# A decoder step in split float32: other gaps between the weight buffers and the operand tiles in SBUF

## The chip, the cores and the metric

The kernel runs on one core of a Trainium2 chip. The metric is the device time of one execution in microseconds; lower is better. Beside the times there is a profile of one execution, taken by the hardware profiler.

## What is computed

One inference step through two layers of a decoder, for a prompt of 256 positions and 8 samples of one position each, 264 columns in all, that share every weight. In short:

```python
def moba_gmlp_mixer(x, ...):          # layer 0
    z = rmsnorm(x, norm_g) @ w_in     # 1024 -> 2560: q, k, v, bu, bv
    a = moba_attention(q, k_all, v_all, pos)
    b_out = spatial_gating(gelu(bu), layer_norm(gelu(bv), sgu_gain), sgu_w, sgu_b)
    return x + concatenate([a, b_out]) @ w_out

def sb_pool_mixer(x, ...):            # layer 1
    z = rmsnorm(x, norm_g) @ w_in     # 1024 -> 2048: q, k, v, u
    c_out = stick_breaking_attention(q, k_all, v_all, pos)
    d_out = pool_mixer(pool_prev, u, pos, pool_w, pool_scale)
    return x + concatenate([c_out, d_out]) @ w_out

def conv_ffn(x, ...):                 # behind each mixer
    h = rmsnorm(x, norm_g)
    g = h @ w_gate                    # 1024 -> 2816
    a = gelu(causal_conv3(g)) * (h @ w_up)
    return x + a @ w_down             # 2816 -> 1024
```

A last rmsnorm follows. Everything is float32, and the caches and states of the samples are read and written besides.

## The kernel before

**Products.** Each large weight matrix is cut into blocks of 128 x 128, 1472 in all, and the activations lie transposed, 128 features by 264 columns. To keep float32 precision with TensorE's faster float32 form (F32R), each operand is split into a high part (h) and the rest (l), and each block takes three products that add up in one PSUM bank: l with xh, then h with xl, then h with xh (`run`, in the list `three`; in the first 30 blocks of layer 0 another order). A product is one load of 128 x 128 weights and one matmul of 264 columns; the profile shows both under L219, the line of the wrapper `TensorE.matmul`, as PEld and PE. The 1472 x 3 products follow one another without a loop in the program; ScalarE and VectorE split the weights of coming blocks meanwhile (L315, L320) and work on finished banks.

**The order of blocks** is fixed by `_phases`: projection in, out, gate and up (ff), and down (dn) of layer 0, then of layer 1, with 160, 64, 352, 176, 128, 64, 352 and 176 blocks. Within one, `m` is the output tile and `k` the input tile. In most of them k runs 0, 1, 2, ... for one m. Exceptions that the prediction uses: in dn the odd m take k from 2 to 21 and then 0 and 1; in the output projections the first 24 blocks take one k for four m in turn, k = 4, 5, 6, 7, 0, 1, and the next 8 take k = 2, 3 for each of these four m. There `catB` holds k = 4 to 7 and `catA` k = 0 to 3.

**Where operands lie.** SBUF is handed out pool by pool, in the order of the lines that open the pools: `con`, `rawp` (weights as loaded), `wsh` (four buffers of high parts), `gap1`, `wsl` (four buffers of low parts), `gap2`, `up` (24 buffers for most else: operand tiles, early weights, cache pages), then `pp` and `sm`. The pools gap1 and gap2 each hold one tile that nothing uses. A weight tile holds 8 blocks, each 128 columns wide and padded to WP = 144; block i of the program is block c = i mod 8 of its tile. An operand tile holds four rows (k mod 4), each 264 columns padded to TP = 272, and starts X0 = 7 columns in:

```python
WP = 144
X0 = 7
    def mv(name):
        return [f4(f"{name}_{x}", (P, 4, TP), F32R)[:, :, X0:X0 + T] for x in "hl"]
    def hl(tiles, k):
        return tiles[k // 4][0][:, k % 4, :], tiles[k // 4][1][:, k % 4, :]
```

The operand tiles are called xg (normalised input), catA and catB (mixer outputs) and a (gated activations), with _h and _l for the parts; wh and wl are the split weights.

Of the kernel before, what the change touches and what calls it, by code (L numbers as in the profile page):

```python
# [9 lines left out]
F32 = mybir.dt.float32  # L10
# [8 lines left out]
P = 128  # L19
# [187 lines left out]
def tile_decoder_step(ctx: ExitStack, tc: tile.TileContext, a):  # L207
# [21 lines left out]
    gap1 = ctx.enter_context(tc.tile_pool(name="gap1", bufs=1))  # L229
    wsl = ctx.enter_context(tc.tile_pool(name="wsl", bufs=4))  # L230
    gap2 = ctx.enter_context(tc.tile_pool(name="gap2", bufs=1))
# [48 lines left out]
    def late(dst, src):  # L280
        tc.keep_in_program_order(nc.sync.dma_start(dst, src))

    gap1.tile([P, 56], F32, name="gap1")
    gap2.tile([P, 32], F32, name="gap2")

    def wtiles(tt):
        return [p.tile([P, 8, WP], F32R, tag=f"w{x}", name=f"w{x}{tt}")[:, :, :P] for p, x in ((wsh, "h"), (wsl, "l"))]
# [1052 lines left out]
```

## Time and profile before

| | before |
|---|---|
| median of three runs | 590.23 us (589.93 to 590.53) |
| the profiled execution | 590.45 us, of it the span 588.7 us |
| granted TensorE clock, mean | 0.999 |
| HBM read and written | 117.65 MB and 3.96 MB |

The span runs from the first instruction to the last. A busy share is the part of the span in which an engine had an instruction under way. Matmuls are pipelined: one starts while the one before still drains, so the durations of single matmuls overlap and their sum exceeds the span. What one costs is the time from its start to the next one's start. In the chain of work that ended last, each step is followed back to what released it; a piece such as "115.50 190.29 PE mm L219 x1578" tells its start, its length, and how many instructions were merged into it. Rows of groups show "busy us, mean ns of one".

### The profile page before, as it was taken

The page shows a single profiled execution, that of the slowest core. Times are in us where ns is not written, and L with a number is a line of the kernel's source. Part 1 is how long each engine was busy: PE and PEld are TensorE (multiplying, and loading weights), DVE is VectorE, ACT ScalarE, POOL GpSimd, SP SyncE. Part 2 cuts the span into 40 slices and gives each one's busy share as a digit, 9 for nine tenths or more (in the row PEclk, how much of TensorE's full clock was granted, in tenths as well). Part 3 has the DMA queues.
Part 4 walks back from the last instruction along what each step waited for, and adds up shares of the span by engine and source line. Part 5 has one row for each costly group of instructions (what it writes and reads, how often), then busy time and mean ns, then how long its engine had stood idle before and what let it go on. Part 6 is the DMA issues. An engine that isn't in the chain of part 4 may idle for free.

```text
span 588.7 us, 12306 instructions
## 1 busy us (share of the span) xinstructions
PE 583.5 (99%) x4909; PEld 568.8 (97%) x4909; DVE 419.7 (71%) x740; ACT 344.5 (59%) x615; POOL 113.2 (19%) x108
## 2 busy tenths in 40 slices
PE   9999999999999999999999999999999999999997
PEld 8998979999999999999999897999999999999996
DVE  6999766878777777665659585588777777764442
ACT  7848955775555555644453476667656565665442
POOL 1410021222222222210120000132232323221010
PEclk9999999999999999999999999999999999999999
DMA  8997973554454545795567865254545454546501
GB/s 318 370 368 284 380 265 102 186 172 187 168 191 161 197 169 190 270 398 199 178 230 258 279 227 187 81 209 151 209 148 211 148 211 146 207 161 219 208 2 73
DMA packets 27707, 122.40 MB, mean 208 GB/s; under 512 B 3330, under 2 KB 4226, under 8 KB 16258
## 3 DMA queue, kind: packets, MB, share of 16 engines
q1 hardware_dynamic: 27648, 121.62, 57.3%
q8 instruction: 38, 0.62, 0.4%
q14 instruction: 19, 0.16, 0.1%
q10 hardware_dynamic: 2, 0.00, 0.0%
HBM read 117.65 MB, written 3.96 MB: 207 GB/s over the span
## 4 chain that ended last, share of the span: by engine, by line
PE 96%; ACT 1%; DMA 1%; DVE 0%; SPq 0%; issue 0%; DVEq 0%
PE mm L219 89%; PE sc L219 1%; PE pv_l L219 1%; PE pav L219 1%; DMA xw<-in_xw 1%; PE pt L222 1%; PE S L219 1%; PE Z L219 1%; ACT xg_h L421 0%; ACT wh L750 0%; DVE wl L751 0%; PE pf L219 0%; PE pm L219 0%; PE vtp_v L222 0%; SPq L386 0%; ACT wh L738 0%
## 5 line engine op out<-in xcount | busy, mean ns | idle before, releaser
L320 DVE TENSOR_TENSOR wl<-raw,wh 128x1024 fp32r<-128x1024 f32 x179 | 219.3, 1227 | 69.5 <-ACT wh L315 69.1
L315 ACT ACTIVATE wh<-raw 128x1024 fp32r<-128x1024 f32 x179 | 187.6, 1051 | 84.0 <-PE mm L219 75.7
L219 PE MATMUL mm<-xg_f_l,wh 128*128 128x264 f32 x704 | 198.5, 282 | 0.0
L219 PE MATMUL mm<-xg_f_h,wh 128*128 128x264 f32 x704 | 198.2, 282 | 0.0
L219 PE MATMUL mm<-xg_f_h,wl 128*128 128x264 f32 x704 | 198.0, 281 | 0.0
L219 PEld LDWEIGHTS mm<-xg_f_h,wl 128*128 128x128 f32 x704 | 132.7, 188 | 0.0
L219 PEld LDWEIGHTS mm<-xg_f_l,wh 128*128 128x128 f32 x704 | 131.7, 187 | 0.0
L219 PEld LDWEIGHTS mm<-xg_f_h,wh 128*128 128x128 f32 x704 | 131.6, 187 | 0.0
L613 POOL TENSOR_TENSOR wk<-wk 128x264 f32<-128x264 f32 x44 | 66.3, 1507 | 194.6 <-DVE wk L612 148.0
L219 PE MATMUL mm<-a_l,wh 128*128 128x264 f32 x352 | 99.3, 282 | 0.0
L219 PE MATMUL mm<-a_h,wh 128*128 128x264 f32 x352 | 99.1, 282 | 0.0
L219 PE MATMUL mm<-a_h,wl 128*128 128x264 f32 x352 | 99.1, 281 | 0.0
L219 PEld LDWEIGHTS mm<-a_h,wl 128*128 128x128 f32 x352 | 66.4, 189 | 0.0
L219 PEld LDWEIGHTS mm<-a_h,wh 128*128 128x128 f32 x352 | 65.9, 187 | 0.0
L219 PEld LDWEIGHTS mm<-a_l,wh 128*128 128x128 f32 x352 | 65.9, 187 | 0.0
L470 ACT ACTIVATE a_h<-wk 128x264 fp32r<-128x264 f32 x44 | 18.6, 424 | 73.8 <-POOL wk L613 73.8
L471 DVE TENSOR_TENSOR a_l<-wk,a_h 128x264 fp32r<-128x264 f32 x44 | 19.2, 437 | 42.0 <-ACT a_h L470 42.0
L219 PE MATMUL mm<-xg_h,wl 128*128 128x264 f32 x160 | 43.2, 292 | 0.2 <-DVE wl L751 0.2
L219 PE MATMUL mm<-xg_h,wh 128*128 128x264 f32 x160 | 42.6, 288 | 0.1
L219 PE MATMUL mm<-xg_l,wh 128*128 128x264 f32 x160 | 41.9, 283 | 0.0
L219 PE MATMUL mm<-xg_n_h,wl 128*128 128x264 f32 x128 | 37.8, 295 | 0.0
L219 PE MATMUL mm<-xg_n_h,wh 128*128 128x264 f32 x128 | 36.1, 282 | 0.0
(265 smaller groups left out, 900.0 us busy)
## 6 DMA issues: line engine op xcount, KB each, us to landing
raw<-in_w SPq DMA_DIRECT2D x89, 1024.0 KB, 4.9
K<-in_kt SPq DMA_DIRECT2D x32, 256.0 KB, 6.5
V<-in_vp SPq DMA_DIRECT2D x32, 256.0 KB, 6.4
raw<-in_w SPq DMA_DIRECT2D x3, 512.0 KB, 6.5
xw<-in_xw SPq DMA_DIRECT2D x3, 388.0 KB, 6.0
X<-in_x SPq DMA_DIRECT2D x4, 264.0 KB, 6.6
out_y<-y SPq DMA_DIRECT2D x3, 256.0 KB, 2.2
out_k<-k SPq DMA_DIRECT2D x1, 528.0 KB, 7.3
```

What stands on the lines that cost most here:

```text
L219: return self.keep(nc.tensor.matmul(*x, **k))
L222: return self.keep(nc.tensor.transpose(*x, **k))
L315: i = s.activation(h, src, AF.Copy)
L320: i = v.tensor_tensor(l, src, h.bitcast(F32), ALU.subtract)
L470: s.activation(h, src, AF.Copy)
L471: v.tensor_tensor(l, src, h.bitcast(F32), ALU.subtract)
L613: g.tensor_tensor(A, A, C, ALU.mult)
```

## The change

Two numbers change, the sizes of the two unused tiles, in float32 elements:

```diff
-    gap1.tile([P, 56], F32, name="gap1")
-    gap2.tile([P, 32], F32, name="gap2")
+    gap1.tile([P, 48], F32, name="gap1")
+    gap2.tile([P, 8], F32, name="gap2")
```

So in each partition the low weight parts move down by 32 bytes against the high ones, and `up`, `pp` and `sm` by 128 bytes. With the sizes above, x then lies 252 bytes, modulo 256, ahead of the weights that are loaded for the next product, for all three products of a block in which c and k agree modulo 4; before, these distances are 124, 124 and 92. No instruction is added, removed or moved on any engine, and no tile gets another size or another number of buffers.

## The prediction

> **What bounds the kernel now.** I read the page's busy shares first, then what TensorE waits for, then the chain that ended last.
>
> ```profile
> span 588.7 us, 12306 instructions
> PE 583.5 (99%) x4909; PEld 568.8 (97%) x4909; DVE 419.7 (71%) x740; ACT 344.5 (59%) x615; POOL 113.2 (19%) x108
> PEclk9999999999999999999999999999999999999999
> PE 96%; ACT 1%; DMA 1%; DVE 0%; SPq 0%; issue 0%; DVEq 0%
> PE mm L219 89%; PE sc L219 1%; PE pv_l L219 1%; PE pav L219 1%; DMA xw<-in_xw 1%; PE pt L222 1%; PE S L219 1%; PE Z L219 1%; ACT xg_h L421 0%; ACT wh L750 0%; DVE wl L751 0%; PE pf L219 0%; PE pm L219 0%; PE vtp_v L222 0%; SPq L386 0%; ACT wh L738 0%
> PE warm L219 <- PEq L1306: 0.8, 1, 0.8
> PE mm L219 <- DVE wl L751: 0.2, 1, 0.2
> ```
>
> TensorE is busy throughout at the full granted clock, it holds 96% of the chain, and its two rows of waits come to 1.0 us. No other engine needs watching. 89% of the span is one kind of work: the split products of L219, of which there are 1472 blocks x 3 = 4416. So the kernel's time is the number of products times the time from the start of one to the start of the next. Two long pieces of the chain give that step:
>
> ```profile
> 115.50 190.29 PE mm L219 x1578
> 396.19 185.22 PE mm L219 x1536
> ```
>
> 190.29 / 1578 and 185.22 / 1536 are both 120.6 ns. The change can matter only through these 120.6 ns, or through the short stretches that are not products.
>
> **What the change moves.** Every engine issues the same instructions in the same order before and after; only addresses differ, so no count and no queue enters the sum. All distances below are remainders by 256 bytes. A weight tile is 8 x 144 x 4 = 4608 bytes and a tile of `up` 4352 bytes, both whole multiples of 256, so every buffer of a pool has its pool's remainder. Call that of `wsh` 0. Then `wsl` goes from 224 to 192, and `up` from 224 + 128 = 96 (less 256) to 192 + 32 = 224. Block c of a weight tile lies 64 c further (144 x 4 = 576), row k of an operand tile 28 + 64 k further. Where c and k agree by remainder 4, as in about 1370 of the 1472 blocks, the three products of a block have x ahead of the weights that are loaded for the next product by:
>
> - first (weights l, operand xh; next h): 28 + 96 = 124 before, 252 after
> - second (h, xl; next h again): 124 before, 252 after
> - third (h, xh; next is l of block c + 1): 28 + 96 - 224 - 64 = 92 before, 252 after
>
> Does the trace say that this distance matters? It holds other distances already, in the blocks where c and k disagree. In the down projections the odd output tiles end with k = 0 and 1. The first projection of that kind starts with block 576; its second output tile has those two at blocks 618 and 619, where c is 2 and 3: two ahead, so the distances are 252, 252 and 220. Block 618 is 126 products after the first, at 236.87 + 126 x 0.1206 = 252.06 us:
>
> ```profile
> 236.87 0.28 PE L219 MATMUL mm<-a_h,wl 128*128 128x264 f32 x1
> ...
> 252.06 0.28 PE L219 MATMUL mm<-a_h,wl 128*128 128x264 f32 x1
> ```
>
> The view that groups lines gives the mean duration in the window 252.22 to 252.78 us, which holds just these six products, and in 253.68 to 254.23 us, which holds six with the usual distances:
>
> ```profile
> L219 PE MATMUL mm<-a_h,wh 128*128 128x264 f32 x2 | 0.6, 285 | 0.0
> L219 PE MATMUL mm<-a_l,wh 128*128 128x264 f32 x2 | 0.6, 284 | 0.0
> L219 PE MATMUL mm<-a_h,wl 128*128 128x264 f32 x2 | 0.6, 281 | 0.0
> ```
>
> ```profile
> L219 PE MATMUL mm<-a_l,wh 128*128 128x264 f32 x2 | 0.6, 282 | 0.0
> L219 PE MATMUL mm<-a_h,wl 128*128 128x264 f32 x2 | 0.6, 282 | 0.0
> L219 PE MATMUL mm<-a_h,wh 128*128 128x264 f32 x2 | 0.6, 282 | 0.0
> ```
>
> The loads that run beside them show it as well. Here are the rows of weight loads of those two windows, the unusual distances first:
>
> ```profile
> L219 PEld LDWEIGHTS mm<-a_h,wl 128*128 128x128 f32 x2 | 0.4, 190 | 0.0
> ...
> L219 PEld LDWEIGHTS mm<-a_h,wl 128*128 128x128 f32 x2 | 0.4, 188 | 0.0
> ```
>
> So a product and the load of the next weights do hinder each other, by a few nanoseconds, and the distance changes by how much. A duration is some 161 ns longer than the step (about 282 against 120.6), since it goes on while the next product streams; a nanosecond more of one I count as a nanosecond more of the other.
>
> The Trainium skill (TensorE: Matmul & The Clock Gate, "Step-by-step: what each phase is for") says that TensorE has two independent read ports into SBUF, so that loading the next weights takes no read bandwidth from the running product. The rows above (281 to 285 against 282, loads of 190 against 188) speak against it at this fine grain; by that rule alone the change would do nothing.
>
> **The sum.** By these rows, against the usual block:
>
> - First product at 252: 281 against 282, so -1 ns.
> - Second at 252: 284 against 282, so +2 ns.
> - Third at 252: the trace has no row of it. Below, it could be like the first at 252, -1 ns. Above, it could be like the third at 220, the nearest distance that there is, 285 against 282, so +3 ns. I take the middle, +1 ns, since one row has the right distance and the other the right product; both ends stay for the range.
>
> That is +2 ns a block, between 0 and +4, and x 1370 blocks: **+2.7 us, between 0 and +5.5**. The hundred blocks with other distances keep their mix, moved by 128 or so, and are put at nothing (the two in each odd tile of the down projections get 124, 124 and 124; 16 blocks x 5 ns are under 0.1 us).
>
> The other term is the data that moves along. Everything in `up` and behind it moves by 128 bytes, among it the tiles that the first loads fill, and the chain has one of these loads:
>
> ```profile
> 2.60 5.48 DMA xw<-in_xw
> raw<-in_w SPq DMA_DIRECT2D x89, 1024.0 KB, 4.9
> raw<-in_w SPq DMA_DIRECT2D x3, 512.0 KB, 6.5
> ```
>
> By the addresses that the program is built with, the 89 loads go to tiles that start 160 bytes behind a multiple of 256, the 3 to tiles in `up` that start on one, and 128 behind it after the change; the former are no slower for their size, so I put this at nothing. A twentieth of the 5.48 us in either direction would be 0.3 us. VectorE, ScalarE and GpSimd read the same tiles at moved addresses; TensorE hides them, having waited for one of them for 0.2 us in all.
>
> The profiled execution took 590.45 us: 588.7 of span and 1.75 around it, 0.2 above the median of 590.23. From the median, 590.23 + 2.7 = **593.0 us**.
>
> **The rivals.**
>
> *No change.* If what a load takes from a product is the same at every distance, only at another moment, the sum of a block stays. For it: the first two products at 252 come to 565 ns together against 564, so all of the forecast beyond 1 ns hangs on the third. Then 590.2, within 1.2 us.
>
> *Faster.* One distance for all three may settle into one rhythm, in which every product starts as the good ones do. For it: the first product at 252 is below its usual duration in the rows above, and single products come down to 279 (window 253.92 to 253.99 us):
>
> ```profile
> L219 PE MATMUL mm<-a_h,wh 128*128 128x264 f32 x1 | 0.3, 279 | 0.0
> ```
>
> Against it: the first product at 252 was followed by a slow one at the same distance. If all three were like the first, -3 ns x 1370 = -4.1 us: 586.1. If all were at 279, -3 x 3 x 1370 ns = -12 us: 578, the end of what this trace has. It decides at the point where the third product at 252 is more than 1 ns below its usual 282.
>
> The Trainium skill (the same page, "Back-to-back issue gap") gives N / 2.4 + 2.5 ns for products one behind the other, 112.5 ns for 264 columns, against the 120.6 ns measured. If the 8 ns between were all hindrance and 252 removed it, an estimate from that page would be 33 us less; no row here comes near it, since the shortest product is 3 ns below the usual one.
>
> *Clearly slower.* Slow products at 252 may feed each other when no good distance comes in between. The trace has a stretch of it. In the first output projection, the first product on catA is block 176, where c = 0; blocks 183, 184 and 185 are then three in a row at 252, 252, 220. They start seven blocks later and end where block 186 starts:
>
> ```profile
> 91.94 0.28 PE L219 MATMUL mm<-catA_h,wl 128*128 128x264 f32 x1
> ...
> 94.46 0.28 PE L219 MATMUL mm<-catA_h,wl 128*128 128x264 f32 x1
> ...
> 95.56 0.28 PE L219 MATMUL mm<-catA_h,wl 128*128 128x264 f32 x1
> ```
>
> 1.10 us / 9 is 122.2 ns a product, 1.6 more than 120.6 (within 1 ns for the rounding). 1.6 x 3 x 1370 is +6.6 us: 596.8. The worst single products, the second and third of block 618 (window 252.35 to 252.42 us), would, if all were so, give +4.5 x 4110 ns = +18 us: 609.
>
> ```profile
> L219 PE MATMUL mm<-a_l,wh 128*128 128x264 f32 x1 | 0.3, 287 | 0.0
> L219 PE MATMUL mm<-a_h,wh 128*128 128x264 f32 x1 | 0.3, 286 | 0.0
> ```
>
> **How the numbers follow.** The forecast, 0 to +4 ns a block with most of it above +1, gets 0.42 and the stretch at 252 with +6.6 us or more 0.14; no change 0.20; faster 0.24. A measurement of this kernel can tell some 0.2% from no change, 1.2 us. The forecast's lowest part falls within that and counts to "same" in exchange for what "no change" spreads upward, so faster 0.25, same 0.20, slower 0.55. The range has to reach the faster case at 586 and the slower one just past 597; all products at 279, and all at 286, are left out: 586 to 598.
>
> **What would show it.** The steps of the two long pieces of the chain in the changed profile: 121.3 ns for the forecast, 120.6 for no change, under 120.2 for faster, 122 for clearly slower. The mean durations by group: the wl group (first product) near 281, the second, on the l operand, near 284, the third near 283. The rest of the span should not move: the pieces sc, pv, pav and the start up to the first product within 0.3 us. I am wrong if the third product goes the other way than its neighbour at 220, or if the three settle into a rhythm that short stretches between other distances cannot show.

## The result, and the profile after

The changed kernel takes 587.02 us (586.67 to 587.46), the kernel before 590.23 us: a ratio of 0.9947, 95% interval 0.9933 to 0.9962. It is 0.5% faster, where 0.5% slower was forecast. The time is inside the range, near the rival "faster" (586.1).

The first page of the changed kernel, beside the lines shown of before:

```profile
span 585.6 us, 12306 instructions
PE 579.7 (99%) x4909; PEld 563.7 (96%) x4909; DVE 420.1 (72%) x740; ACT 344.3 (59%) x615; POOL 114.1 (19%) x108
PE 73%; DVE 13%; ACT 7%; POOL 4%; issue 2%; DMA 1%; SPq 0%; DVEq 0%; POOLq 0%; ACTq 0%
```

TensorE is as busy as before, but its share of the chain fell from 96% to 73%: somewhere the chain now leaves it. The span is 3.1 us shorter. The pieces of the chain say how fast the products follow one another, in their order of time:

```profile
115.21 86.01 PE mm L219 x720
243.47 60.73 PE mm L219 x506
394.16 86.01 PE mm L219 x720
522.42 55.71 PE mm L219 x464
```

86.01 / 720 is **119.5 ns** a product, against 120.6 before. All three products of a block got quicker: by the starts in the trace, in blocks in which c and k agree, the step behind the first fell from 120.4 to 119.6 ns, behind the second from 120.5 to 119.2, behind the third from 120.8 to 119.6. The mean durations in the groups of the page show less of it (last number; before they were 281 for the first, wl, and 282 for the other two):

```profile
L219 PE MATMUL mm<-xg_f_h,wh 128*128 128x264 f32 x704 | 197.8, 281 | 0.0
L219 PE MATMUL mm<-xg_f_h,wl 128*128 128x264 f32 x704 | 197.8, 281 | 0.0
L219 PE MATMUL mm<-xg_f_l,wh 128*128 128x264 f32 x704 | 197.5, 280 | 0.0
```

1.1 ns x 4110 products would be 4.5 us, and 3.1 came. The long piece of 1578 products that stood in the chain of before is now broken: at 201 us the chain leaves TensorE for the work on the last gated activation, and at 243 us it comes back. The timeline of TensorE there, and of VectorE, shows why (start us, length us, and in brackets the idle time before and what ended it):

```profile
242.85 0.28 PE L219 MATMUL mm<-a_h,wh 128*128 128x264 f32 x1
243.00 0.39 PE L219 MATMUL mm<-a_h,wl 128*128 128x264 f32 x1
243.47 0.39 PE L219 MATMUL mm<-a_l,wh 128*128 128x264 f32 x1
243.69 0.28 PE L219 MATMUL mm<-a_h,wh 128*128 128x264 f32 x1
242.98 0.43 DVE L471 TENSOR_TENSOR a_l<-wk,a_h 128x264 fp32r<-128x264 f32 x1 [1.10 <-ACT a_h L470]
```

The end of the first output tile of the down projection needs the last gated activation, a_l, which VectorE finishes at 243.41. From 243.00 to 243.69 there are two products that take 0.24 at the usual step: some 0.45 us of stall. In the kernel before VectorE wrote it from 243.36 to 243.79:

```profile
243.36 0.43 DVE L471 TENSOR_TENSOR a_l<-wk,a_h 128x264 fp32r<-128x264 f32 x1 [1.10 <-ACT a_h L470]
```

There TensorE came to it only at 236.87 + 63 x 0.1206 = 244.5. It is now there 1.5 us earlier, at 243.00, and a_l only 0.4. Both layers have this wait in the changed kernel, and the view of waits, on the row of weight loads, has it as new:

```profile
PEld mm L219 <- DVE a_l L471: 0.6, 2, 0.3
```

### The profile page after: what moved, and what is told of

Read it like the earlier page. It is cut to its first block, busy times and chain, and to the rows that moved or that the text cites. A ratio compares the mean times of both kernels' runs of the same rounds, so it can differ in the third digit from the quotient of the medians.

```text
span 585.6 us, 12306 instructions
## 1 busy us (share of the span) xinstructions
PE 579.7 (99%) x4909; PEld 563.7 (96%) x4909; DVE 420.1 (72%) x740; ACT 344.3 (59%) x615; POOL 114.1 (19%) x108
## 4 chain that ended last, share of the span: by engine, by line
PE 73%; DVE 13%; ACT 7%; POOL 4%; issue 2%; DMA 1%; SPq 0%; DVEq 0%; POOLq 0%; ACTq 0%
PE mm L219 67%; DVE wl L320 6%; POOL wk L613 4%; ACT wh L315 3%; PE pv_l L219 1%; DVE wk L604 1%; DVE wk L612 1%; PE pav L219 1%; DVE wk L603 1%; DMA xw<-in_xw 1%; ACT p L865 1%; PE sc L219 1%; PE Z L219 1%; ACT p L868 0%; PE pt L222 0%
## 5 line engine op out<-in xcount | busy, mean ns | idle before, releaser
L219 PE MATMUL mm<-xg_f_h,wh 128*128 128x264 f32 x704 | 197.8, 281 | 0.0
L219 PE MATMUL mm<-xg_f_h,wl 128*128 128x264 f32 x704 | 197.8, 281 | 0.0
L219 PE MATMUL mm<-xg_f_l,wh 128*128 128x264 f32 x704 | 197.5, 280 | 0.0
L219 PEld LDWEIGHTS mm<-xg_f_h,wh 128*128 128x128 f32 x704 | 131.9, 187 | 0.0
L219 PEld LDWEIGHTS mm<-xg_f_h,wl 128*128 128x128 f32 x704 | 131.9, 187 | 0.0
L219 PEld LDWEIGHTS mm<-xg_f_l,wh 128*128 128x128 f32 x704 | 131.9, 187 | 0.0
L219 PE MATMUL mm<-a_h,wl 128*128 128x264 f32 x352 | 99.1, 282 | 0.0
L219 PE MATMUL mm<-a_l,wh 128*128 128x264 f32 x352 | 98.9, 281 | 0.2
L219 PE MATMUL mm<-a_h,wh 128*128 128x264 f32 x352 | 98.9, 281 | 0.0
L219 PEld LDWEIGHTS mm<-a_l,wh 128*128 128x128 f32 x352 | 66.0, 187 | 0.6 <-DVE a_l L471 0.6
L219 PEld LDWEIGHTS mm<-a_h,wl 128*128 128x128 f32 x352 | 65.9, 187 | 0.2
L219 PEld LDWEIGHTS mm<-a_h,wh 128*128 128x128 f32 x352 | 65.9, 187 | 0.0
L219 PE MATMUL mm<-xg_h,wl 128*128 128x264 f32 x160 | 43.0, 291 | 0.5 <-DVE wl L751 0.5
L219 PE MATMUL mm<-xg_h,wh 128*128 128x264 f32 x160 | 41.9, 283 | 0.0
L219 PE MATMUL mm<-xg_l,wh 128*128 128x264 f32 x160 | 41.7, 282 | 0.0
L219 PE MATMUL mm<-xg_n_h,wl 128*128 128x264 f32 x128 | 37.7, 295 | 0.0
L219 PE MATMUL mm<-xg_n_h,wh 128*128 128x264 f32 x128 | 36.0, 282 | 0.0
```

Of the source, the lines that this page charges most:

```text
L219: return self.keep(nc.tensor.matmul(*x, **k))
```

## The experiments

In all of them only unused tiles, X0 or an order differ from one of the two kernels. Distances are those of the first, second and third product, for blocks in which c and k agree.

### Half the change, and moves that keep the distances

`x_only` moves the operand tiles to 252 and leaves the low weights:

```diff
-    gap2.tile([P, 32], F32, name="gap2")
+    gap2.tile([P, 64], F32, name="gap2")
```

> The gaps are 56 and 64: x moves to 252 from the high weights, the low weights stay where they were, so the distances are 252, 252, 220. If the prediction's rows held for long stretches too (slow third product at 220 that also disturbs its neighbours), the step in the long pieces is 121.3 to 122.2 ns and the time 593 to 597 us: slower than before although two of three products have the new distance. If moving x to 252 brings the gain whatever the third product has, the step is near 119.7 ns and the time near 587.5 us.

It took 589.81 us, ratio 0.9993 (0.9984 to 1.0002): no gain, and no loss either. Its long piece is "115.12 190.21 PE mm L219 x1578", 120.5 ns. This is the run that judges the prediction's rows. It has 252, 252 and 220 in one block after the other, and in the down projection (window 254.22 to 254.67 us) they read:

```profile
L219 PE MATMUL mm<-a_l,wh 128*128 128x264 f32 x2 | 0.6, 282 | 0.0
L219 PE MATMUL mm<-a_h,wl 128*128 128x264 f32 x2 | 0.6, 282 | 0.0
L219 PE MATMUL mm<-a_h,wh 128*128 128x264 f32 x2 | 0.6, 281 | 0.0
```

In the short stretch of before the same three distances read 284 (a_l), 281 (wl) and 285 (a_h,wh). So these distances do not fix the duration; what went before counts too. Both expectations fell: neither 593 nor 587.5.

Even a stretch that lasts does not settle it. In the output and first gate and up products the same run has 252, 252, 220 in one block after the other as well, and there (window 100 to 114 us) the chain has

```profile
99.95 14.10 PE mm L219 x118
```

which is 119.5 ns, the step of the changed kernel. It ends at 115 us, where two small products of the norm (ns_f) come between; behind them the step is 120.5 ns.

`all_124` moves the low weights alone:

```diff
-    gap1.tile([P, 56], F32, name="gap1")
-    gap2.tile([P, 32], F32, name="gap2")
+    gap1.tile([P, 48], F32, name="gap1")
+    gap2.tile([P, 40], F32, name="gap2")
```

> The gaps are 48 and 40: only the low weights move, and the distances are 124, 124, 124. If it is one distance for all three that helps, whatever its value, the step is near 119.5 ns and the time near 587 us. If it is the value 252, the step stays at 120.2 to 120.6 ns and the time at 589 to 590 us. The short stretches at 124, 124, 124 in the changed kernel (the mean duration of the six products is 281.3) point to some 120.2 ns.

590.08 us, ratio 0.9997 (0.9988 to 1.0006); the piece is "115.02 190.21 PE mm L219 x1578", 120.5 ns. One distance for all three is not enough by itself.

`up_256` is the changed kernel with gap2 of 72 in place of 8, `moved_128` the kernel before with 128 unused bytes in front:

```diff
     PT = con.tile([1, NS * NPG], I32, name="PT")
+    con.tile([P, 32], F32, name="pad")
```

> The changed kernel with everything behind the weights moved by another 256 bytes (gaps 48 and 72): the same distances by remainder. If only distances modulo 256 matter, 587 us within 0.6 and a step of 119.5 ns. If a longer period or the addresses themselves matter, the step differs by half a nanosecond or more.

> The kernel before with 128 bytes of unused tile in front, so that all split weights, operand tiles and their neighbours move by 128 bytes together and the distances stay at 124, 124, 92. If only distances matter, 590.2 us within 0.6 and a step of 120.6 ns. If the gain of the change came from the place of the operand tiles, which lie 128 bytes further here as there, 587 us.

They took 587.33 us (0.9950, 0.9936 to 0.9963) and 590.04 us (0.9999, 0.9990 to 1.0008). Their pieces, first of `up_256`, then of `moved_128`:

```profile
114.70 71.68 PE mm L219 x600
```

```profile
115.41 190.29 PE mm L219 x1578
```

That is 119.5 ns as in the changed kernel, and 120.6 as before. So the relative place decides between the two kernels: the kernel before stays slow when all of this moves by 128 bytes, and the changed one stays quick when the operand tiles and what lies behind them move by 256. The changed kernel moved as a whole by less than 256 bytes was not run.

### Other distances, alike for all three

Each is the changed kernel with one number changed: X0 = 8, 6 or 3 for 0, 248 and 236, gap2 = 64, 16, 24 or 56 for 220, 28, 60 and 188.

> The changed kernel with X0 = 8: every operand row starts 4 bytes later, the distances are 0, 0, 0. If 252 is good because x starts just short of the next weights' place, 0 loses it: a step of 120.2 ns or more, 589 us or more. If only the coarse place within 256 bytes matters (steps of 16 or 32 bytes), 587 us as at 252.

> The changed kernel with X0 = 6: distances of 248. A smooth dependence on the distance gives about the step of 252, 119.5 ns, and 587 us; a sharp place at 252 gives 120.2 ns and 589 us or more.

> The changed kernel with X0 = 3: 236 for all three, 16 bytes below 252. 248, 252 and 0 gave steps of 122.1, 119.5 and 120.6 ns. If the fine pattern repeats every 16 bytes, 236 is like 252 and 220: a step of 119.5 to 119.9 ns and 587 to 588 us. If it repeats every 32 bytes, 236 is unlike both, 120.5 ns or more and 590 us or more.

> The changed kernel with the operand tiles 32 bytes lower (gaps 48 and 64): 220 for all three. By the prediction's row (the third product at 220 was the slowest) the step is 121 ns or more and the time 592 us or more. By the run in which only x was moved, where the third product at 220 was the quickest of the three (119.9 ns), the step is 120.0 ns and the time 588 to 589 us.

> One distance of 28 for all three (gaps 48 and 16), 32 above 252. If the coarse place matters little as long as all three share it, as at 220, the step is 119.5 to 120.0 ns and the time 587 to 588 us. If it rises away from 252 as it does at 124 (120.55 ns), 120 ns or more, 588.5 us or more.

> One distance of 60 (gaps 48 and 24). The short stretches of six to seven blocks at 60, 60, 60 in the changed kernel have products of 120, 120, 120 ns; if short stretches told what long ones do, the step is 120.0 to 120.2 ns and the time 588.5 to 589.5 us. If they mislead, as they did at 252, something else by half a nanosecond or more.

> One distance of 188 (gaps 48 and 56), between 220 (119.8 ns) and 124 (120.55 ns). A smooth dependence gives 120.0 to 120.3 ns and 588.5 to 589.5 us; the short stretches at 188 in the changed kernel give 120.0 (three blocks) and 121.1 (seven).

The table gives the long piece of the chain of each run, its length over its number of products, and the step that follows from it.

| distance | long piece, us / products | step, ns | time, us | ratio to before (95%) |
|---|---|---|---|---|
| 124, 124, 92 (before) | 190.29 / 1578 | 120.6 | 590.23 | |
| 252, 252, 220 | 190.21 / 1578 | 120.5, at first 119.5 | 589.81 | 0.9993 (0.9984 to 1.0002) |
| 252 (the change) | 86.01 / 720 | 119.5 | 587.02 | 0.9947 (0.9933 to 0.9962) |
| 0 | 190.33 / 1578 | 120.6 | 590.61 | 1.0009 (1.0000 to 1.0018) |
| 248 | 192.18 / 1578 | 121.8 in the mean of 120.6 and 125.0 | 596.93 | 1.0111 (1.0095 to 1.0126) |
| 236 | 191.96 / 1578 | 121.6 | 594.44 | 1.0074 (1.0057 to 1.0091) |
| 220 | 189.18 / 1578 | 119.9 | 587.51 | 0.9955 (0.9941 to 0.9968) |
| 188 | 71.69 / 600 | 119.5, then 120.6 | 588.97 | 0.9978 (0.9968 to 0.9988) |
| 124 | 190.21 / 1578 | 120.5 | 590.08 | 0.9997 (0.9988 to 1.0006) |
| 60 | 189.38 / 1578 | 120.0 | 588.07 | 0.9966 (0.9952 to 0.9980) |
| 28 | 190.20 / 1578 | 120.5 | 590.15 | 1.0000 (0.9991 to 1.0010) |

Two of these runs have two steps at one and the same distance, each for a hundred products or more. With 248 the chain reads, in the windows 100 to 114, 120 to 236 and 255 to 268 us:

```profile
99.94 14.12 PE mm L219 x113
119.99 116.09 PE mm L219 x963
254.92 13.12 PE mm L219 x105
```

These are 125.0, 120.6 and 125.0 ns. The first passage is again at the two products of the norm. The second is not at the start of the down projection (239 us), whose first blocks keep 120.6 ns, but at 254 to 255 us, at the two blocks in which c and k disagree. With 188, in the windows 120 to 236 and 255 to 268 us:

```profile
119.95 67.03 PE mm L219 x561
254.97 13.14 PE mm L219 x109
```

These are 119.5 and 120.6 ns. The first 60 products of the down projection still have a step of 119.4 ns by their starts; the passage is at the stall on a_l near 243 us, which this run has as the changed kernel does. So the step does not follow from the distance alone: at an interruption it can change, and stay changed. Why it does so there and not at others is open.

Four bytes to either side of 252 lose the gain: 0 is as slow as before, and 248 is, in the mean, slower than the kernel before. Sixteen bytes lower, 236 is slow too, so the pattern does not repeat every 16 bytes. These three runs change X0, and so both the distance and where a row of x starts modulo 32 bytes, which all the other runs leave alone; no run tells the two apart, since none moves the weights by less than 32 bytes. In steps of 32 bytes (28, 60, 124, 188, 220, 252) the time stays between 587 and 590.2 us, not smoothly: 28 and 60, and 28 and 252, are neighbours. For 220 the durations of `x_only` were the better guide: 120.0 ns and 588 to 589 us were expected from them, and the time came out half a microsecond lower. The guess that 28 would be as good as 220 failed, and so did the smooth rise expected of 188. The expectation for 60 held in the step, 120.0 ns; the time, 588.07 us, came out 0.4 below the 588.5 to 589.5 expected. (The 122.1 ns for 248 in the expectation of 236 is a mean over the agreeing blocks of the whole kernel; the long piece alone gives 121.8.)

### The microsecond that was given back

`late_tail` is the changed kernel with the first two output tiles of each down projection taken in turn, in an order in which c and k agree in all but two of their blocks, as before:

```diff
-        ph.append((f"dn{l}", [(m, k) for m in m8 for k in (kf[2:] + kf[:2] if m[1] % 2 else kf)]))
+        a, b = m8[:2]
+        ph.append((f"dn{l}", [(a, k) for k in kf[:12]] + [(b, k) for k in kf[:12]] + [(a, k) for k in kf[12:]] + [(b, k) for k in kf[14:] + kf[12:14]]
+                   + [(m, k) for m in m8[2:] for k in (kf[2:] + kf[:2] if m[1] % 2 else kf)]))
```

> The changed kernel, with another order of the first two output tiles of each down projection: k = 0 to 11 of both first, then the rest of each, so that the last gated activation is needed some 4 us later. If the two stalls of 0.5 us on a_l are what the change gives back there, they vanish: about 1 us less than the changed kernel, 586.0 us. If the stall only moves (to the weight splits or the next gated activation), the time stays at 587.0 us.

586.21 us (585.89 to 586.51), ratio to before 0.9932 (0.9918 to 0.9945): 0.8 us less than the changed kernel, and the fastest of all that ran. The two intervals overlap a little, the times themselves do not, and the trace settles it: no wait for a_l is left, and the long piece is whole again (L221 is the L219 of before, two lines down).

```profile
115.06 188.50 PE mm L221 x1578
393.52 183.48 PE mm L221 x1536
```

188.50 / 1578 is 119.5 ns. Against the 190.29 and 185.22 us of before these two pieces are 1.79 and 1.74 us shorter, which is the 1.1 ns times their products. In the changed kernel the same stretch, from the start of the piece to the next piece at 304.44, was 189.23 us, against 190.54 before (115.50 to 306.04): 1.31 us gained, some 0.5 less.

## Why the prediction was wrong

**What bounds the kernel** was right: in every run the time followed the step of the products. **That the place of x against the weights matters**, and not the place of the data that moves along, was right and is borne out by `moved_128` and `up_256`. The Trainium skill's rule that loading the next weights takes nothing from the running product (TensorE: Matmul & The Clock Gate, "Step-by-step: what each phase is for") would by itself leave the time as it was. The measurement differs: with the same instructions at other addresses, the mean step ran from 119.5 to 121.8 ns. Whether it is read bandwidth that a load takes, no run shows.

**The sum** failed, in two of its three terms and in the step they share. "First product at 252: 281 against 282, so -1 ns" came out as a step (-0.8 ns), though the mean duration was 281 before and after. "Second at 252: 284 against 282, so +2 ns" was read as 280 in the changed kernel, and its step fell by 1.3 ns. "Third at 252 ... I take the middle, +1 ns" was read as 281, and its step fell by 1.2 ns. In steps, the block was forecast at +2 ns and measured at -3.4.

The step behind both terms was to read a steady duration from two blocks that stand alone between others. `x_only` shows the fault: once the distances 252, 252, 220 last, the step is 120.5 ns or even 119.5, not the 121 to 122 of the short stretches. So a product's time depends not only on its own distance but also on the products before it; in what way is open. The prediction named this way of being wrong itself, a rhythm "that short stretches between other distances cannot show". `x_only` also speaks against a sum over single products: over most of that run 252 for two products gains nothing while the third is at 220, 220 for all three gains 2.6 us, and 252 for all three 3.2.

**A nanosecond of duration as a nanosecond of step** was loose too: the xg_f rows fell by 0, 2 and 1 ns, the steps of the three products by 0.8, 1.3 and 1.2.

**The rivals.** "Faster" was right in its direction and near in its size: -3 ns a block and 586.1 us, against -3.4 ns and 587.02 us. Its mechanism, that one distance for all three settles into one quick rhythm, holds for 252 but is neither enough nor needed: 124, 28 and 0 are alike for all three and bring nothing, and in `x_only` 252, 252, 220 ran at 119.5 ns for a while. Its point of decision, a third product more than 1 ns below its usual 282, was passed in the step (-1.2 ns) but not in the mean duration (281). That the range held is owed to this rival, which set its lower end; the forecast itself pointed the other way. "Clearly slower" rested on the same kind of short stretch and did not come; 248 shows that a slow rhythm can last all the same, 125.0 ns. "What would show it" named a step under 120.2 ns, which is what the chain has.

The 112.5 ns that the prediction took from the Trainium skill (TensorE: Matmul & The Clock Gate, "Back-to-back issue gap") were reached in no run. That section gives the formula for an isolated product and says that in a stream with a load for each product both count, so the 8 ns above it need not be hindrance.

**The cover.** The prediction said that no other engine needs watching. That was so of before; 1.5 us of gain was enough to bring TensorE to the last a_l ahead of VectorE, twice, and about 0.5 us was lost each time.

What stays open is the mechanism. The runs show that the relative place matters and that the step can change for long at an interruption, but not by what rule: 252, 220 and 60 are good, 28 and 124 are not, and 188 and 248 have two steps each. For moves by less than 32 bytes it is open whether the distance counts or where the rows of x start.

## What to carry to other kernels

Where TensorE runs one product after the other and each loads its own weights, the place in SBUF of the running operand against the next weights is worth a scan, with all products alike; here it moved the time by 1.7% from best to worst. Read a steady cost only from a stretch that lasts, and from more than one: a block that stands alone among others shows the passage, and two long stretches at the same distance can still differ by what went before. And after a gain on the bounding engine look at which of the others it now has to wait for.

## What was not expected of the hardware

- Four bytes are 9.9 us: 248 takes 596.93 us and 252 takes 587.02.
- Equal distances give mean steps from 119.5 to 121.8 ns at 264 columns, and none of the nine values tried is below 119.5.
- At one distance the step can be 120.6 or 125.0 ns (248), and 119.5 or 120.6 (188), each for a hundred products or more, by what came between.
- The same three distances (252, 252, 220) give mean durations up to 4 ns apart, 285 against 281, by what went before: two blocks alone in the kernel before, a long run in `x_only`.
